# Norms, running sums and output tiles of a two-layer encoder placed among chains of matmuls

## The chip, the cores and the metric

The kernel runs on one core of a Trainium2 chip. It is one inference step, and what is measured is the device time of one execution in microseconds (us). The core has five engines that take their instructions from queues of their own: PE (matmuls, and their weight loads, PEld), DVE (vector work), ACT (activations), POOL (GpSimd: elementwise work here) and SP (here it issues the transfers between memory and the core). An engine takes its queue in order; a semaphore tells it when what another engine makes is there.

## The reference

Two layers work on 2048 tokens of a prompt and 32 tokens of a sample, 1024 numbers each, all in f32:

```python
sh, sc, gt = split(silu(c) @ ada_w[i] + ada_b[i])            # modulation, once per sequence
h = rmsnorm(x, norm_pre[i]) * (1 + sc) + sh
# layer 0: RG-LRU, 12 blocks of 128 channels
xb, gate = split(h @ w_in)                                   # 1024 -> 2 x 1536
xc = conv4(xb); r, ig = sigmoid(xc @ w_a + b_a), sigmoid(xc @ w_x + b_x)
hs = scan(a = exp(-8 r softplus(-lam)), u = sqrt(1 - a*a) * ig * xc)
y = (hs * silu(gate)) @ w_out
# layer 1: forgetting attention, 16 heads of 64
q, k, v, g, fl = split(h @ w_in); log_f = log_sigmoid(fl + b_f)
cum = cumsum(log_f)                                          # the sample starts from 512 cached rows
y = (softmax(q k / 8 + cum_q - cum_k, causal) @ v * silu(g)) @ w_out
x = x + gt * rmsnorm(y, norm_post[i])                        # after each layer
```

Outputs are x of both sequences, the states of layer 0, and k, v and log_f of layer 1.

## The kernel before

Every f32 operand of a product is split into a rounded part (hi) and the rest (lo), and one product is three matmuls, hi·hi, lo·hi and hi·lo. The helpers at L92 to L101 are these splits: `hi` on ACT, POOL or DVE, `lo` always a subtraction on DVE.

The tokens go in two halves of 1024; the second half carries the 32 sample tokens as well. The stages in order of time:

- Setup and modulation of layer 0: `ada` (L227) streams the modulation weights in 512-column pieces, splits them (tiles `scs`) or takes them whole (`scf`) and multiplies at L290. The modulation of layer 1's scale, shift and gate is spread over later stages.
- `prenorm` (L309) of a half: groups of two token tiles of 128 tokens are loaded (L326), ACT takes the sum of squares (L335), DVE and POOL make the factor (L337 to L339) and DVE scales the rows (L342). Then eight blocks per group, one for each 128 of the 1024 channels: two transposes on PE (L361) into a bank of PSUM, ACT scales and shifts it out of the bank (L367), POOL makes hi (L95) and DVE lo (L101). The result is `h`, the moving operand of the layer's products.
- `lru_in` for a half: twelve blocks of weights; for each chunk of up to 512 tokens a chain of 24 matmuls for xb and one of 24 for the gate (L460), then the convolution (L483), the gates' matmuls (L473) and the tail with the scan (L494 to L511) of the block before. The gate weights lie in two slots (`wg`).
- `load_wout` (L566) splits the output weights; `out_tiles` (L586) multiplies each of 17 token tiles by them (L624: 12 pairs of k, six matmuls each), normalizes, adds the residual (L638 to L647) and stores.
- Layer 1: `prenorm` of a half; `proj` (V at L796, then units k, q, g of eight pairs of heads at L825); `forget` and `forget_sums`, whose matmuls at L696 and L697 are the running sums of the log forget values; `attention` as jobs of a pair's head (products at L990, L1024, L1028, L1076, L1077).
- `merge` (L1238) puts the steps of `main()` (projections, then output tiles) beside those of the attention by a ratio of estimated costs, and a last `out_tiles` follows.

Generators write this order: each function yields between steps, and the main body says which is advanced when. A list scheduler behind it may still move an instruction past others, so the order on an engine is not quite the order of the code. Buffers are named pools (`h` 32, `w` 5, `raw` 3, `half` 5, `ahalf` 12, `c` 12, `wg` 2), and the eight banks of PSUM are pj 2, st 2, mx 2, pva 1 and pvb 1. A new tile waits until the last reader of its slot has ended.

At the borders the old order is: all of a half's groups are normalized in runs of eight blocks (the first two groups before the first products, the rest after the first block), out tiles follow one by one, and the second half's norm begins when the first half's `h` comes free.

## Time and profile before

| | us |
|---|---|
| median of three runs (3147.41 to 3154.5) | 3149.36 |
| profiled execution, its own time | 3159.12 |
| its span (first to last instruction) | 3157.4 |
| PE busy in the span | 2935.5 (93%) |
| PEld | 2340.3 (74%) |
| DVE | 1921.4 (61%) |
| ACT | 1425.5 (45%) |
| POOL | 1372.6 (43%) |

PE is busy nearly all the time, so its time is read in two steps: how long it was busy in a stretch, and which share of its full clock it was granted meanwhile. The share is in the column PEclk of the windows (1.00 is the upper level, 2.4 GHz, 0.50 the lower, 1.2 GHz; what lies between is a mixture). A stretch without waits at full clock has PE busy for all of it and 1.00.

### The profile page before, as it was taken

The page shows a single profiled execution, that of the slowest core. Times are in us where ns is not written, and L with a number is a line of the kernel's source. Part 1 is how long each engine was busy: PE and PEld are TensorE (multiplying, and loading weights), DVE is VectorE, ACT ScalarE, POOL GpSimd, SP SyncE. Part 2 cuts the span into 40 slices and gives each one's busy share as a digit, 9 for nine tenths or more (in the row PEclk, how much of TensorE's full clock was granted, in tenths as well). Part 3 has the DMA queues.
Part 4 walks back from the last instruction along what each step waited for, and adds up shares of the span by engine and source line. Part 5 has one row for each costly group of instructions (what it writes and reads, how often), then busy time and mean ns, then how long its engine had stood idle before and what let it go on. Part 6 is the DMA issues. An engine that isn't in the chain of part 4 may idle for free.

```text
span 3157.4 us, 45059 instructions
## 1 busy us (share of the span) xinstructions
PE 2935.5 (93%) x14900; PEld 2340.3 (74%) x14900; DVE 1921.4 (61%) x3387; ACT 1425.5 (45%) x2884; POOL 1372.6 (43%) x1449
## 2 busy tenths in 40 slices
PE   7999899998999999999998989999999989888988
PEld 3777678896678877777776777777878777766667
DVE  7787657757322556554655747676676766675732
ACT  4455555555111424343435616464555646454621
POOL 6444243323121534343444515564555555454632
PEclk9999889999999999999999889999999999988999
DMA  8545424333533476776757563455455445444333
GB/s 280 170 166 183 167 96 137 125 131 120 176 91 117 158 240 183 223 201 198 213 191 215 158 205 91 132 160 155 123 151 148 129 132 141 134 135 116 84 99 117
DMA packets 341432, 488.72 MB, mean 155 GB/s; under 512 B 79112, under 2 KB 191880, under 8 KB 341200
## 3 DMA queue, kind: packets, MB, share of 16 engines
q1 hardware_dynamic: 341200, 485.85, 50.3%
q8 instruction: 118, 1.93, 0.3%
q14 instruction: 114, 0.93, 0.1%
HBM read 307.57 MB, written 178.14 MB: 154 GB/s over the span
## 4 chain that ended last, share of the span: by engine, by line
PE 28%; issue 6%; DVE 6%; DMA 5%; POOL 3%; ACT 2%; SPq 1%; POOLq 0%; DVEq 0%; ACTq 0%
PE pj L825 8%; PE st L1024 3%; PE pva L1076 3%; PE mx L990 3%; PE st L1028 3%; PE pvb L1077 2%; PE pj L796 2%; PE pj L624 2%; DVE ahalf L101 1%; POOL ahalf L1053 1%; DVE mxs L993 1%; POOL half L646 1%; DMA dns_d<-rc 1%; ACT ahalf L1030 1%; DVE half L101 1%
## 5 line engine op out<-in xcount | busy, mean ns | idle before, releaser
L1053 POOL TENSOR_TENSOR ahalf<-ahalf,ahalf 128x512 f32<-128x512 f32 (+2 forms) x528 | 578.4, 1095 | 321.0 <-ACT ahalf L1030 296.1
L825 PE MATMUL pj<-h,w 128*128 128x512 f32 (+1 forms) x2304 | 597.4, 367 | 9.3 <-DVE w L101 8.0
L101 DVE TENSOR_TENSOR ahalf<-st,ahalf 128x512 fp32r<-128x512 f32 (+3 forms) x640 | 386.3, 605 | 247.1 <-ACT st L1031 196.1
L1030 ACT ACTIVATE ahalf<-st 128x512 fp32r<-128x512 f32 (+3 forms) x640 | 340.9, 533 | 379.6 <-PE st L1028 333.8
L825 PEld LDWEIGHTS pj<-h,w 128*128 128x128 f32 x2304 | 427.5, 192 | 93.9 <-DVE w L101 9.7
L993 DVE TENSOR_REDUCE mxs<-mx 128x1 f32<-128x512 f32 (+5 forms) x672 | 384.7, 595 | 100.6 <-PE mx L990 71.6
L1031 ACT ACTIVATE st<-st 128x512 f32<-128x512 f32 (+2 forms) x720 | 354.9, 493 | 0.0
L1024 PE MATMUL st<-ahalf,kv 128*128 128x512 f32 (+3 forms) x640 | 251.6, 395 | 50.8 <-DVE ahalf L101 41.1
L990 PE MATMUL mx<-kb,qm 96*128 96x512 f32 (+5 forms) x672 | 250.1, 398 | 19.0 <-DVE mxs L993 14.1
L796 PE MATMUL pj<-w,h 128*128 128x256 f32 (+3 forms) x1296 | 246.0, 294 | 0.0
L1028 PE MATMUL st<-ahalf,kb 96*128 96x512 f32 (+3 forms) x640 | 243.1, 389 | 2.4 <-ACT ahalf L1011 2.0
L1076 PE MATMUL pva<-ahalf,vs 128*128 128x512 f32 (+3 forms) x640 | 235.0, 387 | 6.4 <-ACT ahalf L1030 4.5
L1077 PE MATMUL pvb<-ahalf,vs 128*65 128x512 f32 (+3 forms) x640 | 227.7, 368 | 8.4 <-DVE ahalf L101 7.4
L101 DVE TENSOR_TENSOR ahalf<-ahalf,ahalf 128x512 fp32r<-128x512 f32 (+1 forms) x163 | 142.5, 877 | 148.8 <-PE st L624 97.0
L101 DVE TENSOR_TENSOR half<-half,half 128x256 fp32r<-128x256 f32 (+3 forms) x160 | 140.3, 877 | 150.3 <-POOL half L95 142.7
L95 POOL TENSOR_SCALAR half<-half 128x256 fp32r<-128x256 f32 (+3 forms) x160 | 85.5, 535 | 330.4 <-ACT half L833 127.2
L460 PE MATMUL pj<-h,w 128*128 128x512 f32 (+1 forms) x1056 | 228.2, 367 | 0.8 <-POOL h L95 0.7
L460 PEld LDWEIGHTS pj<-h,w 128*128 128x128 f32 x1056 | 182.9, 192 | 36.0 <-POOL h L95 1.2
L796 PEld LDWEIGHTS pj<-w,h 128*128 128x128 f32 (+1 forms) x1296 | 197.5, 190 | 12.5 <-ACT half L367 0.2
L1024 PEld LDWEIGHTS st<-ahalf,kv 128*128 128x128 f32 x640 | 123.0, 192 | 98.9 <-DVE ahalf L101 64.4
L624 PE MATMUL pj<-h,w 128*128 128x512 f32 (+1 forms) x624 | 180.3, 427 | 14.7 <-DVE half L645 9.2
L825 PE MATMUL pj<-h,raw 128*128 128x272 f32 (+1 forms) x576 | 191.6, 333 | 0.0
(315 smaller groups left out, 5733.2 us busy)
## 6 DMA issues: line engine op xcount, KB each, us to landing
wp_d<-w SPq DMA_DIRECT2D x60, 512.0 KB
vs<-v_d SPq DMA_DIRECT2D x96, 256.0 KB
kv<-k_d SPq DMA_DIRECT2D x192, 128.0 KB
ahalf<-q_d SPq DMA_DIRECT2D x192, 128.0 KB
raw<-in_w SPq DMA_DIRECT2D x44, 512.0 KB
ahalf<-in_ada_w SPq DMA_DIRECT2D x64, 256.0 KB
v_d<-half SPq DMA_DIRECT2D x64, 256.0 KB
w<-wp_d SPq DMA_DIRECT2D x30, 512.0 KB
```

The source lines that it names most:

```text
L101: dve.tensor_tensor(o, i, f(h), ALU.subtract)
L460: pe.matmul(ps[:, :b - a], l, cols(r, a, b), start=i == 0, stop=i == 23)
L796: pe.matmul(ps[:m, :nw], l, r, start=c == 0, stop=c == 23)
L825: pe.matmul(ps[:, :b - a], l, cols(r, a, b), start=c == 0, stop=c == 23)
L990: pe.matmul(ps[:sw, :kw], u.qm[0:96, s0:s0 + sw], kb, start=True, stop=not last)
L993: dve.tensor_reduce(u.mxs[:sw, si, c:c + 1], ps[:sw, :kw], axis=AX.X, op=ALU.max)
L1024: pe.matmul(ps[:kw, c0:nq], j.ka[k0 // 512][:, kc:kc + kw], u.qa[:, c0:nq], start=True, stop=False)
L1028: pe.matmul(ps[:kw, c0:nq], j.kb[k0 // HALF][0:96, kd:kd + kw], u.qb[0:96, c0:nq], start=False, stop=True)
L1030: act.activation(ph[:kw, c0:nq], ps[:kw, c0:nq], AF.Exp, scale=0.125)
L1031: act.activation(ps[:kw, c0:nq], ps[:kw, c0:nq], AF.Exp, scale=0.125)
L1053: pool.tensor_tensor(u.acc[:kw, c0:nq], f(ph)[:kw, c0:nq], u.acc[:kw, c0:nq], ALU.add)
L1076: pe.matmul(u.pva[:, c:nq], vs[:kw, 0:128], ph[:kw, c:nq], start=ti == 0, stop=last)
```

## The change

The norm gets a written plan. `prenorm` reads a string: `L01` loads groups 0 and 1, `S01` makes their statistics and scales them, `R01:a` runs their blocks for the first four k (`:b` for the last four), `Y` gives the turn back. A function says in which pool each row lies, and a block is one step. `weave(gen, other, n)` advances `other` by n steps behind each step of `gen`; `take` advances a generator by a number of steps.

- *Start.* `ada` for scale and shift is cut in two: pieces 0 and 2 run first, 1 and 3 between the blocks of groups 0 and 1. The first block's chains come in quarters (two k each), xb and gate in turn, between the blocks of the second four k. Groups 2 and 3 are woven into the second chunk.
- *Half switch of layer 0.* Loads, statistics and scaling of the second half's first groups stand before or in the last block; its second chunk is woven with two blocks behind each quarter chain. Chunks of half 1 are cut 512, 256, 288 and no longer 512, 272, 272.
- *Modulation of layer 1's gate* moves from the out tiles (whole f32 products) into the modulation that runs beside the chains (split products).
- *Out tiles, layer 0.* The first two tiles run together on each pair of weights, in four banks. The norm of layer 1's first half is woven into the last tile's twelve steps and into the first sixteen steps of V.
- *Running sums.* Their DVE part (`prepare`) stands at the end of V; the matmuls come after the first k unit, those of the sample after the first q unit.
- *Half switch of layer 1.* Statistics before the last unit; two blocks behind each of its steps, then one behind each of 24 steps of V.
- *Attention and end.* In half 1 the sample's two jobs come before the pair's long ones. `main()` does seven out tiles in place of eight; the last call does tile 7, tiles 8 to 15 and the sample tile, in place of the sample tile and 8 to 15.

```diff
-ADA_FIRST, ADA_LAST = 8, 6
-
-NORM_AT, NORM_WITH = 15 * 12, 8
-
-V_STEPS = 8
+ADA_FIRST = 8
+
+NORM_AT, NORM_WITH = 14 * 12, 12
...
-    return [(0, 512), (512, 784), (784, 1056)]
+    return [(0, 512), (512, 768), (768, 1056)]
...
-    def prenorm(layer, half, src, h, bank, xn_role=lambda g: "xn"):
+    def prenorm(layer, half, src, h, bank, plan, row, by_k=False):
...
+        for step in plan.split():
+            gs = [int(c) for c in step[1:].split(":")[0]]
+            if step[0] == "L":
+                load(gs)
+            elif step[0] == "S":
+                stats(gs)
+            elif step[0] == "Y":
+                yield 0.0
+            else:
+                ks = range(4, KD) if step.endswith("b") else range(4) if step.endswith("a") else range(KD)
+                for gi, k in [(gi, k) for k in ks for gi in gs] if by_k else [(gi, k) for gi in gs for k in ks]:
+                    yield block(gi, k)
+                if not step.endswith("a"):
+                    flags.update(("n", layer, half, gi) for gi in gs)
...
+    def weave(gen, other, n):
+
+        i = 0
+        while True:
+            try:
+                x = next(gen)
+            except StopIteration as e:
+                return e.value
+            yield x
+            for _ in range(n[i % len(n)]):
+                x = next(other, None)
+                if x is not None:
+                    yield x
+            i += 1
+
+    def take(gen, n):
+        for _ in range(n):
+            x = next(gen, None)
+            if x is not None:
+                yield x
...
-        def chain(ps, wh, wl, a, b):
-            i = 0
-            for k in range(KD):
+        def chain(ps, wh, wl, a, b, ks):
+            for k in ks:
                 lh = wh[:, 128 * k:128 * k + 128]
                 ll = wl[:, 128 * k:128 * k + 128]
-                for l, r in ((lh, h[0][k]), (lh, h[1][k]), (ll, h[0][k])):
-                    pe.matmul(ps[:, :b - a], l, cols(r, a, b), start=i == 0, stop=i == 23)
-                    i += 1
+                for i, (l, r) in enumerate(((lh, h[0][k]), (lh, h[1][k]), (ll, h[0][k]))):
+                    pe.matmul(ps[:, :b - a], l, cols(r, a, b), start=k + i == 0, stop=k == KD - 1 and i == 2)
...
+            if n == NB - 1:
+                flags.add(("last", 0, half))
+                yield 0.0
...
-                ps = bank()
-                chain(ps, wxh, wxl, a, b)
-                for (u, v, c) in spans(a, b):
-                    act.activation(xb[:, 3 + c:3 + c + v - u], ps[:, u:v], AF.Copy)
-                ps = bank()
-                chain(ps, wgh, wgl, a, b)
+                px, pg = bank(), bank()
+                first = n == 0 and ci == 0
+                parts = [(px, wxh, wxl), (pg, wgh, wgl)]
+                order = [(q, p) for q in range(4) for p in parts] if first else [(q, p) for p in parts for q in range(4)]
+                for i, (q, p) in enumerate(order):
+                    chain(*p, a, b, (2 * q, 2 * q + 1))
+                    if q == 3 and p is parts[0]:
+                        for (u, v, c) in spans(a, b):
+                            act.activation(xb[:, 3 + c:3 + c + v - u], px[:, u:v], AF.Copy)
+                    if i < 7:
+                        yield 0.0
+                ps = pg
+                del px, pg, p, parts, order
...
+        groups = [[i] for i in range(len(tiles))]
+        if both:
+            groups[0:2] = [[0, 1]]
+        for i in groups[0]:
+            load(i)
+            split(i)
+        for gi, g in enumerate(groups):
+            nxt = groups[gi + 1] if gi + 1 < len(groups) else []
+            for i in nxt:
+                load(i)
+            pss = [[bank(), bank()] for _ in g]
+            xs = []
+            for k in range(kn):
+                wh, wl = w[0][k], w[1][k]
+                for i, ps in zip(g, pss):
+                    m = rows(tiles[i])
+                    o = zq[i][k // kz]
+                    zh, zl = o[0][:, k % kz, :], o[1][:, k % kz, :]
+                    for c, (l, r) in enumerate(((zh, wh), (zh, wl), (zl, wh))):
+                        for n in range(2):
+                            pe.matmul(ps[n][:m, :], l, r[n], start=k + c == 0, stop=k == kn - 1 and c == 2)
...
-        sums(fl, lsum, [128] * 8, ext_d, HALF * half)
+        parts = prepare(fl, lsum, 8)
+        yield
+        sums(parts, [128] * 8, ext_d, HALF * half)
+        del parts
...
-                if kind == "k" and p == 0:
-                    forget_sums(half, fl, bank)
-                    yield 2000.0
+                if kind in "kq" and p == 0 and ("f", half) not in flags:
+                    next(fsum, None)
...
+                for sample in ((True, False) if half else (False,)):
...
-        pre = prenorm(0, 0, io["x"], h, bank1)
+
+        pre = prenorm(0, 0, io["x"], h, bank1, "L01 S01 Y R01:a L23 R01:b S23 Y R23",
+                      lambda g, t: ("xn", "xn") if g < 2 else ("aw", "xn"), by_k=True)
         next(pre)
-        run(ada(0, (0, 2, 1, 3), bank0, bank0, ADA_FIRST, lambda i: i % 3 == 0))
+        mod = ada(0, (0, 2, 1, 3), bank0, bank0, ADA_FIRST, lambda i: i % 3 == 0)
+        left = [lambda: None, lambda: None]
+        blocks = lru_in(0, h, bank0, bank1, lc, left)
+        run(take(mod, 2 * KD))
+        for i in range(KD):
+            run(take(mod, 2))
+            run(take(pre, 1))
+            if i == KD // 2:
+                next(blocks)
+        run(mod)
+        next(blocks)
+        for _ in range(4):
+            run(take(pre, 2))
+            next(blocks)
+        run(until(pre, ("n", 0, 0, 0)))
...
             yield from ada(1, (0, 1, 2, 3), bpvb, bank0)
+            yield from ada(1, (4, 5), bpvb, bank0)
...
+        run(take(weave(take(blocks, 4), pre, (4, 4, 4, 4)), 99))
+        run(pre)
+        run(side(until(blocks, ("last", 0, 0))))
+        h = new_h()
+        pre = prenorm(0, 1, io["x"], h, bank1, "L01 S01 L2 Y R01:a S2 R01:b L3 Y R2 L4 S3 Y R3 S4 R4",
+                      lambda g, t: {(0, 0): "raw", (0, 1): "raw", (1, 0): "raw", (2, 1): "w"}.get((g, t), ("xn", "xn")),
+                      by_k=True)
+        next(pre)
+        second_half = lru_in(1, h, bank0, bank1, lc, left)
+        next(second_half)
+        run(until(blocks, ("free", 0, 0, 0)))
+        run(weave(blocks, pre, (2,)))
+        run(until(pre, ("n", 0, 1, 0)))
+        blocks = second_half
+        run(take(blocks, 2))
+        run(weave(take(blocks, 7), pre, (1, 2)))
+        run(until(pre, ("n", 0, 1, 2)))
+        run(weave(side(take(blocks, 8)), pre, (2,)))
+        run(pre)
+        run(side(until(blocks, ("free", 0, 1, 0))))
         for _ in range(4):
             next(wout)
-        for fn in rest:
+        run(blocks)
+        run(mod)
...
+        pre = prenorm(1, 0, x1_d, h, bank1, "L0 S0 L1 Y S1 R0 L2 R1 S2 L3 Y R2 S3 R3",
+                      lambda g, t: "wg" if g % 2 == 1 else "any")
+        set_roles(big, "half", N_HALF, "z")
+        out = out_tiles(list(range(8)) + [16] + list(range(8, 16)), NB, z_d, io["x"], x1_d, gps, bank0, w, both=True)
+        n_out = 16 * NB
+        run(take(out, NORM_AT))
+        next(pre)
+        run(take(out, n_out - NORM_AT - NORM_WITH))
+        run(weave(out, pre, (1,)))
         del w, gps, out
         run(until(pre, ("n", 1, 0, 1)))
         pbank = [bank0]
         first_half = proj(0, h, lambda: pbank[0]())
-        for part in (until(pre, ("n", 1, 0, 2)), pre):
-            for _ in range(V_STEPS):
-                next(first_half)
-            run(part)
+        run(weave(take(first_half, 16), pre, (1,)))
+        run(pre)
...
+        yield from until(a, ("last", 1, 0))
+        pre = prenorm(1, 1, x1_d, hb, bpj, "L0 S0 L1 Y S1 R0 L2 R1 Y S2 R2 L3 L4 S3 S4 R34",
+                      lambda g, t: "raw" if g == 0 or (g, t) == (1, 0) else ("hf", "hf") if g == 4 else "w")
+        next(pre)
         yield from until(a, ("free", 1, 0, 0))
-        pre = prenorm(1, 1, x1_d, hb, bpj, lambda g: "raw" if g % 2 else "w")
+        yield from weave(a, pre, (2,))
         yield from until(pre, ("n", 1, 1, 1))
-        yield from a
+        yield from weave(take(b, 24), pre, (1,))
...
-        yield from out_tiles(list(range(8)), NP, z2_d, x1_d, y_o, gps, bpj, w, False)
+        yield from out_tiles(list(range(7)), NP, z2_d, x1_d, y_o, gps, bpj, w, False)
...
-    run(out_tiles([16] + list(range(8, 16)), NP, z2_d, x1_d, y_o, att["gps"], cycle(bpj, bpj, bst, bst), att["w"]))
+    run(out_tiles([7] + list(range(8, 17)), NP, z2_d, x1_d, y_o, att["gps"], cycle(bpj, bpj, bst, bst), att["w"]))
```

On PE at the half switch of layer 0, before (st and pj are banks with a chain of products, `ident` marks a transpose, `scs` a modulation product):

```order
L460 MATMUL st_3259<-h_839,wg_2791 128x512
L460 MATMUL st_3259<-h_840,wg_2791 128x512
L460 MATMUL st_3259<-h_839,wg_2792 128x512
L290 MATMUL pvb_2513<-ahalf_2997,scs 34x512
L290 MATMUL pvb_2513<-ahalf_2998,scs 34x512
L361 MATMUL pva_3055<-ident,ahalf_3005 128x128
L361 MATMUL mx_3064<-ident,ahalf_3005 128x128
L361 MATMUL mx_3073<-ident,ahalf_3005 128x128
```

The first transposes of the second half follow the last product of the first half's last chain. After the change, in the last block's second chunk:

```order
L361 MATMUL mx_3068<-ident,raw_2927 128x128
L361 MATMUL mx_3068<-ident,ahalf_2929 128x128
L497 MATMUL pj_3051<-h_775,w_2792 128x512
L497 MATMUL pj_3051<-h_791,w_2791 128x512
L497 MATMUL pj_3051<-h_792,w_2791 128x512
L497 MATMUL pj_3051<-h_791,w_2792 128x512
L361 MATMUL mx_3081<-ident,raw_2923 128x128
L361 MATMUL mx_3081<-ident,raw_2925 128x128
L361 MATMUL pva_3090<-ident,raw_2927 128x128
```

Products of the last chains (L460, now L497) stand between the transposes.

On DVE at the same place, before (c tiles belong to the last blocks of `lru_in`, ss and rs to the norm):

```order
L101 TENSOR_TENSOR c_3293<-c_3287,c_3292 128x1024
L533 COPY c_3520<-convc 128x3
L534 COPY c_3520<-cst 128x3
L535 MEMSET c_3520 128x1
L497 SCALAR_TENSOR_TENSOR c_3297<-c_2975,c_3297 128x1024
L337 TENSOR_TENSOR ss_3021<-ss_3021 128x2
L338 TENSOR_SCALAR rs_3022<-ss_3021 128x2
L342 TENSOR_SCALAR ahalf_3005<-ahalf_3005,rs_3022 128x512
```

The norm's factor and its scaling stand behind the convolution and part of the tail of the last blocks. After the change:

```order
L592 TENSOR_TENSOR c_2544<-c_2544,st_2652 128x512
L99 TENSOR_TENSOR wg_2610<-raw_2396,wg_2609 128x1024
L99 TENSOR_TENSOR c_2719<-c_2713,c_2718 128x1024
L571 MEMSET c_2735 128x3
L533 SCALAR_TENSOR_TENSOR c_2723<-c_2621,c_2723 128x1024
L345 TENSOR_SCALAR rs_2934<-ss_2933 128x2
L349 TENSOR_SCALAR raw_2923<-raw_2923,rs_2934 128x1024
L349 TENSOR_SCALAR raw_2925<-raw_2925,rs_2934 128x1024
```

The scaling (now L349, whole rows) stands one block earlier, ahead of the last block's own work (c_2735).

## Rows read from the trace of the kernel before

**Rows 1.** Windows by stage: length; busy us (instructions) per engine; PEclk, DMA share, GB/s

```profile
80.00:370.00 290.00, 289.00 (x1243) 229.25 (x1242) 220.47 (x196) 140.66 (x162) 117.53 (x82) 1.00 0.52 176
0.00:80.00 80.00, 57.28 (x209) 28.89 (x210) 61.86 (x141) 34.18 (x75) 54.43 (x77) 0.91 0.80 279
370.00:440.00 70.00, 48.07 (x199) 34.27 (x198) 40.54 (x85) 45.10 (x92) 29.76 (x50) 0.71 0.27 89
750.00:860.00 110.00, 96.72 (x350) 65.40 (x351) 59.13 (x78) 37.44 (x59) 28.90 (x23) 0.91 0.57 177
1060.00:1140.00 80.00, 73.20 (x442) 64.08 (x441) 46.97 (x105) 27.09 (x57) 41.59 (x71) 0.96 0.62 216
1140.00:1720.00 580.00, 541.50 (x2818) 431.14 (x2817) 338.05 (x624) 239.62 (x514) 247.21 (x271) 0.99 0.67 204
1720.00:1900.00 180.00, 158.68 (x877) 130.08 (x876) 104.39 (x242) 74.38 (x159) 65.44 (x99) 0.86 0.61 179
2780.00:3060.00 280.00, 246.92 (x1050) 182.26 (x1051) 164.07 (x321) 129.13 (x303) 141.72 (x145) 0.90 0.38 104
```

**Rows 2.** Timeline of PE at the start: begin, duration, instruction, [wait <- releaser]

```profile
12.26 0.47 PE L361 MATMUL mx<-ident,ahalf 128*128 128x128 f32 x1 [12.26 <-DVE ahalf L342]
...
54.68 7.02 PE L460 MATMUL pj<-h,w 128*128 128x512 f32 x24
```

**Rows 3.** Windows of 10 us at the start

```profile
30.00:40.00 10.00, 9.75 (x41) 3.37 (x40) 9.04 (x15) 2.86 (x6) 10.00 (x10) 1.00 1.01 380
40.00:50.00 10.00, 4.61 (x18) 1.87 (x18) 9.93 (x15) 2.23 (x5) 10.00 (x8) 0.85 0.38 109
```

**Rows 4.** Groups by form, 20 to 58 us: count | busy, mean ns | idle before

```profile
L101 DVE TENSOR_TENSOR c<-h,c 128x512 fp32r<-128x512 f32 x18 | 15.8, 906 | 1.0 <-PE pj L290 0.5 <-POOL c L95 0.4
...
L95 POOL TENSOR_SCALAR h<-ahalf 128x256 fp32r<-128x256 f32 x16 | 11.7, 752 | 0.0
...
L101 DVE TENSOR_TENSOR h<-ahalf,h 128x256 fp32r<-128x256 f32 x16 | 9.3, 639 | 0.3 <-POOL h L95 0.3
```

**Rows 5.** Timeline of DVE at the half switch of layer 0

```profile
384.45 1.67 DVE L342 TENSOR_SCALAR ahalf<-ahalf,rs 128x512 f32<-128x512 f32 x4 [0.80 <-POOL rs L339]
...
391.21 0.41 DVE L101 TENSOR_TENSOR h<-ahalf,h 128x256 fp32r<-128x256 f32 x1
```

**Rows 6.** Waits of PE, 370 to 440 us: us in total, times, longest

```profile
PE pva L361 <- DVE ahalf L342: 9.2, 1, 9.2
PE mx L361 <- ACT ahalf L367: 6.3, 5, 2.3
PE pva L361 <- ACT ahalf L367: 6.0, 3, 2.7
```

**Rows 7.** PE groups by form over the span: the later modulation

```profile
L290 PE MATMUL pvb<-ahalf,scs 128*34 128x512 f32 x96 | 30.2, 394 | 0.0
...
L290 PE MATMUL pvb<-ahalf,scf 128*34 128x512 f32 x32 | 15.4, 599 | 0.0
```

**Rows 8.** Windows of 10 us at the entry of the out tiles

```profile
760.00:770.00 10.00, 10.00 (x44) 7.32 (x42) 9.96 (x12) 7.79 (x12) 3.57 (x4) 1.00 0.31 105
770.00:780.00 10.00, 5.58 (x12) 2.75 (x11) 10.00 (x9) 5.08 (x6) 7.89 (x4) 0.71 0.46 159
```

**Rows 9.** Window of 20 us at the half switch of layer 1

```profile
1840.00:1860.00 20.00, 11.51 (x65) 9.14 (x66) 10.75 (x39) 0.40 (x1) 0.42 (x1) 0.57 0.58 178
```

**Rows 10.** Waits of PE, 1680 to 1900 us

```profile
PE pj L696 <- DVE fg L98: 7.4, 2, 4.2
```

**Rows 11.** Timeline of PE at the end

```profile
3029.23 12.91 PE L624 MATMUL pj<-h,w 128*128 128x512 f32 x48 [2.91 <-DVE half L645]
...
3047.19 12.84 PE L624 MATMUL pj<-h,w 128*32 128x512 f32 x48 [5.05 <-ACT w L92]
```

**Rows 12.** Windows of 10 us: transposes among modulation products, and among out tiles' products

```profile
420.00:430.00 10.00, 7.90 (x27) 5.24 (x27) 6.16 (x17) 7.09 (x18) 6.57 (x14) 0.50 0.08 19
1090.00:1100.00 10.00, 9.98 (x76) 9.70 (x75) 8.52 (x21) 6.38 (x15) 7.62 (x15) 0.92 0.39 142
```

242 lines of the change are left out of this document (111 added, 131 removed).

## The prediction

> **What bounds the kernel now.** The windows by stage come first. Each row gives PE's busy time and the clock it was granted; a stretch's length less busy time times clock is what it lost against a full-clock PE that never waits. In 80:370, the dense middle of layer 0's first half, that is 290 − 289.0 × 1.00 = 1.0 us, and 1243 matmuls in 289 us make 0.23 us for one (mostly 512 columns). Where stages meet, the rows [rows 1] give:
> - 0:80 (start): 80 − 57.28 × 0.91 = 27.9
> - 370:440 (half switch, layer 0): 70 − 48.07 × 0.71 = 35.9
> - 750:860 (entry of the out tiles): 22.0
> - 1060:1140 (layer change): 9.7
> - 1720:1900 (half switch, layer 1): 43.5
> - 2780:3060 (end of attention): 57.8, while the ordinary mix of 1140:1720 loses 43.9 of 580, 7.6%.
>
> So PE is the bound and the borders are where it is not fed. Then the waits and timelines of each border say what came last there.
>
> **The change, part by part.** The instruction work is nearly the same (17 more PE rows of 14,700), so each term is a share of a border's loss.
>
> *1, start.* The first transpose runs at 12.26 [rows 2]: that much of the 27.9 is load and setup, which stay. 15.6 are in play. The first product chain ran whole at 54.68, after the modulation. Now it comes in quarters, between the halves of the norm's blocks, and two modulation slices precede the other two. Half of the chain's 48 products, 5.5 us, can run in time that PE waited, and about 2.5 of the wait in 40:50 (PE 4.61 of 10) goes with it: 8 us. Against more: DVE and POOL are at 9 to 10 of 10 from 30 to 50 [rows 3], and what they split is the same, so they go on setting this stretch's end. The loads of token groups 2 and 3 now stand on SP's queue behind all of block 0's split weights; the chunk that needs them runs a whole chunk later, 11 us, which covers them. If that cover fails the term is nothing. Bounds 0 and 15.6.
>
> In 20:58 the same split of 128x256 took 639 ns on DVE with POOL's `hi` at 752 ns beside it [rows 4], and 0.41 us when POOL was idle [rows 5]. The Trainium skill ("SBUF — State Buffer", SBUF: two separate sides) says that a DVE operation with two SBUF inputs and a GpSimd operation that reads SBUF exclude each other through one port pair. By that rule the two engines are one resource here and no order of PE's work helps: the term would be 0 to 2 and the sum 67. The rows bear it in direction (the slower pair), not as a full lock, since both ran above 9 of 10 busy.
>
> *2, half switch of layer 0.* PE waited 9.2 us for the first normalized tile, then 6.3 and 6.0 for the ScalarE copies that give the transposes' banks back [rows 6]; with 0.3 of small ones 21.8, the remaining 14 is the clock (0.71). The first wait is DVE's doing: L342 ran at 384.45, behind the tail of the last block, 1.67 us for four, with a wait for POOL's power of 0.80 [rows 5]. Now loads, statistics and scaling of the first groups stand within the last block, and its second chunk has two blocks of transposes behind every six products: 9.2 goes, and most of the bank waits, since 1.4 us of products lies between two pairs. What is late next: block 0's gate weights for half 1 must wait until the last gate chain gives their slots back (1.05 MB at the 380 GB/s of [rows 3], 2.8 us, plus their splits on POOL and DVE), and the last eight blocks of the second group still come without cover. I leave 12 of 35.9 for these: 24 us gained. Bounds 12 (only the waits' half) and 33 (all but the weights).
>
> The Trainium skill ("Perfetto Trace Analysis", Identifying the Most-Contended Engine) holds matmul busy time for a bad measure and takes weight-load busy time instead. By that, dense work loads weights 229.25/290 = 0.79 of the time, 370:440 holds 34.27/0.79 = 43.4 us of such work and lost 26.6, not 35.9; the term would be 15 and the sum 65. I keep the first, since the measured waits and the clock row add up to it.
>
> *3, entry of the out tiles.* The last row before the products is full on DVE (9.96 and 10.00 of 10) while PE falls to 5.58 [rows 8]: the split of the output weights, one pair per k, sets the pace of the first tile. Two tiles on each pair bring 12 × 6 × 0.23 = 16.6 us of products into that stretch. The modulation of layer 1's gates goes from whole f32 products (32 rows, 15.4 us) to split ones (32 rows more, at 30.2/96 = 0.315: 10.1 us) [rows 7]: 5.3 less. Against it: ten of these slices now come after the last chain, and each splits 128x512 on DVE, 10 × 0.9 [rows 4] = 9 us into an engine that is full there. 16.6 + 5.3 − 9 = 12.9, I take 12. Bounds −4 (the splits cost 9 and the second tile is no cover) and 27 (all of the 22.0 and the 5.3).
>
> *4, layer change.* 9.7 lost; the norm's first two groups are woven into the last tile's twelve steps, the rest one block a step into V. The old code did the same in bulk, at a clock of 0.96. I take 4, bounds −4 and 9.7.
>
> *5, half switch of layer 1.* At the ordinary 7.6%, 180 us lose 13.7; the excess is 29.8. Of it 1840:1860 lost 20 − 11.51 × 0.57 = 13.4, with 7.4 us of waits of the running sums of the forget gates for their DVE splits, 2 of them, the longest 4.2 [rows 9, 10]. The first sums keep their place on PE but are prepared at the end of V, a whole k unit earlier; the sample's move behind q. But the longest wait is for the head of a DVE queue that stays: I take 7 of the 13.4. The rest, 16.4, is the bare run of 72 transposes before V; two blocks a step in the last unit and one in 24 V steps take most: 11. Together 18, bounds 5 and 28.
>
> *6, end.* After the last attention matmul the old order has 56 + 432 products, and the tile matmuls at 3029.23 and 3047.19 waited 2.91 and 5.05 and took 12.91 and 12.84 for 48 where 48 × 0.23 makes 11.0 [rows 11]: 11.7 in play. Now tile 7 stands there in place of the small sample tile, which ends the list, so first splits have more cover. The last finish is of 32 rows, not 128, on the same engines. 8, bounds 0 and 12.
>
> *7, attention.* Sample jobs now precede the long ones of each pair; the same units, the same pace rule. The 57.8 of 2780:3060 is 36 above the ordinary share, and nothing added reaches the ScalarE–DVE–POOL chain there. 0, bounds −25 and +15.
>
> Sum: 8 + 24 + 12 + 4 + 18 + 8 + 0 = 74. The profiled execution took 3159.1 us, 9.8 above the median of the runs, 3149.4. 3159.1 − 74 = 3085; on the median's base **3075**.
>
> **The rivals.** (a) *The waits move into the chains.* DVE and POOL have the same splits and scalings to do; woven, each block's wait for its ScalarE copy or its bank stands in front of products, as the waits of 6.3 and 6.0 did [rows 6]. For it: both engines near full at three of the borders. Against: in 80:370 products with the same engines behind them ran dense [rows 1]. Terms 2, 3 and 5 give half or less: about 31, 3118.
>
> (b) *All of it is recovered*: 15.6 + 30 + 20 + 8 + 24 + 8 = 105, 3044. For it: dense stretches lose 0.3%. Against: weights that come late, and stretches bound by DVE.
>
> (c) *Slower: the clock falls in the woven stretches.* Woven products: the last block of half 0 and the first of half 1, 22 and 23 us, the last out tile 17, V's 16 and 24 steps of six half-width products, 11 and 17, the first chain 11: 101 us. At 1.2 in place of 2.4 GHz each costs itself once more. Gains that need no clock: 8 (term 1), 14 (term 2 less 10 of clock), 12, 7 and 8: 49. The change loses once more than 49/101 = 48% of these stretches run at the lower level; at 70% it is 3149.4 + 71 − 49 = 3171. For it: 420:430, transposes between products of the modulation, shows PE busy 7.90 of 10 and a clock of 0.50. Against: 1090:1100, transposes among the out tiles' products, busy 9.98 at 0.92 [rows 12].
>
> (d) *No effect*: DVE and POOL bind at every border and all comes back later: 3149.
>
> **How the numbers follow.** Main case 0.56, (a) 0.20, (b) 0.12, (c) 0.07, (d) 0.05. The main case's own range is 3055 to 3095, some terms at a bound and not all at the same one. For 8 in 10 the range takes in (b) with terms near their upper bounds and (a) down to a third of the gain: 3038 to 3130; left out are (c), (d) and the tails. 0.2% is 6.3 us, about what a measurement of this kernel tells from no change. Faster holds for the main case, (a) and (b): 0.88; same 0.05; slower 0.07.
>
> **What would show it.** After the change, the half switch of layer 0 should hold no wait of PE over 4 us and a clock above 0.85 over its 70 us; the first out tiles should run at PE over 9 of 10; the two sums' waits should be below 4 together; the last tiles should wait under 3. Term 1 is wrong if PE stays under 6 of 10 in a slice before 60 us. The whole is wrong if the lower clock covers woven blocks (c), or if the stages are as short as said and attention between 1900 and 3060 is longer by more than 25 us.

## The result: slower, and where the profile after shows it

The changed kernel took 3186.3 us in the median of three executions, the kernel before, run beside it, 3151.9: by the means 1.0113 of its time, 95% interval 1.0087 to 1.0140. A fourth execution took 9458.5 us for a reason that no trace shows and is left out. 3075 with a range of 3038 to 3130 was predicted; the direction was wrong.

The windows by stage of the changed kernel, in the columns of [rows 1] (length; busy us and instructions of PE, PEld, DVE, ACT, POOL; PEclk, DMA share, GB/s):

```profile
80.00:370.00 290.00, 288.05 (x1236) 226.53 (x1236) 222.71 (x209) 146.04 (x175) 119.87 (x93) 1.00 0.51 174
0.00:80.00 80.00, 53.59 (x188) 24.52 (x188) 56.16 (x132) 29.88 (x66) 45.44 (x65) 0.91 0.75 264
370.00:440.00 70.00, 55.73 (x253) 39.88 (x251) 52.87 (x89) 42.02 (x81) 38.51 (x55) 0.83 0.35 116
750.00:860.00 110.00, 82.40 (x305) 61.29 (x306) 63.44 (x81) 35.04 (x54) 43.46 (x27) 0.80 0.50 159
1060.00:1140.00 80.00, 70.40 (x427) 60.91 (x426) 49.01 (x108) 30.72 (x64) 42.12 (x72) 0.96 0.59 204
1720.00:1900.00 180.00, 154.46 (x850) 124.51 (x850) 100.14 (x235) 75.84 (x165) 66.35 (x104) 0.90 0.55 158
```

Only 370:440 improved by much: it lost 70 − 55.73 × 0.83 = 23.7 where [rows 1] gave 35.9. The start lost 31.2 against 27.9, the entry of the out tiles 44.1 against 22.0, the layer change 12.4 against 9.7, the half switch of layer 1 41.0 against 43.5.

Windows of equal place mislead once a stage has moved, so the rest is read by marks: the start of the same product, counted along the products of one line, in the timelines of both kernels. The table gives the place of each mark and, below a kernel's name, how much longer (+) or shorter (−) than in the kernel before the stretch up to it was. "Three", "l0 in bulk" (bulk_l0) and "scratch" (before_hf) are experiments below.

| mark | before at | changed | three | l0 in bulk | scratch |
|---|---|---|---|---|---|
| 1105th chain product (last block of half 0) | 363.4 | +5.9 | +0.9 | +1.3 | +4.7 |
| 2017th (half 1, seventh block) | 586.8 | −10.4 | −8.1 | −12.9 | −16.2 |
| end of the last chain | 747.9 | +5.0 | +5.8 | +4.8 | −0.1 |
| 289th out-tile product | 856.5 | +7.0 | −29.4 | −26.9 | +1.0 |
| 193rd product of layer 1's projections | 1110.3 | +2.1 | +1.8 | +1.9 | +1.8 |
| 1825th | 1696.1 | +1.2 | −1.6 | −3.2 | −5.5 |
| 2401st (behind the half switch) | 1906.1 | +0.7 | +0.9 | +0.2 | −2.5 |
| end of the last product at L1076 (L1156 in the changed kernel) | 3023.6 | +19.6 | +1.9 | −8.8 | −7.4 |
| end | 3157.4 | +1.8 | −5.9 | −6.5 | −0.2 |
| sum (profiled spans) | | +32.9 | −33.7 | −50.1 | −24.4 |

How exact a mark is: before_jobs below differs from the kernel before only from attention's half 1 on, and its marks agree with it to 1.4 us up to 1696. In attention the same order of instructions can differ by some 10 us (last section), so there the medians decide. A few attention products still follow the last one at L1076: in the kernel before they end 0.8 us behind it, in the changed kernel 4.0. Counted from the very last, the changed kernel's attention is 22.8 us longer and its end 1.4 shorter.

*Entry of the out tiles.* The chains end at 748.5, the first out-tile product starts at 783.1; before it was 747.9 and 749.9. Waits of PE from 748 to 800 us in the changed kernel (total, times, longest):

```profile
PE pvb L288 <- DVE ahalf L99: 7.1, 5, 4.1
PE pvb L288 <- DVE ahalf L251: 7.0, 1, 7.0
PE pj L698 <- DVE ahalf L99: 4.7, 1, 4.7
PE pj L698 <- ACT ahalf L90: 3.2, 1, 3.2
```

and its windows of 10 us there:

```profile
750.00:760.00 10.00, 3.25 (x7) 1.19 (x7) 8.81 (x11) 5.02 (x7) 4.99 (x6) 0.68 0.77 258
760.00:770.00 10.00, 7.05 (x20) 4.66 (x19) 7.63 (x11) 7.24 (x10) 10.00 (x6) 0.50 0.38 115
770.00:780.00 10.00, 4.07 (x9) 1.48 (x8) 10.00 (x12) 4.41 (x7) 6.95 (x5) 0.50 0.30 97
780.00:790.00 10.00, 2.21 (x5) 1.30 (x5) 10.00 (x12) 6.12 (x8) 6.84 (x3) 0.50 0.51 175
```

L288 is the modulation. Ten of its slices (20 products) stand behind the last chain; PE waits for their splits one by one, and once 7.0 us for DVE to read the bank of the piece before (L251), at the lower clock, with DVE full from 770 on. The out tiles' own splits take their tiles from the same pool, `ahalf`, and come last. The timeline of DVE and POOL shows what a split cost there (begin, duration):

```profile
775.42 3.27 POOL L532 TENSOR_TENSOR c<-c,c 128x1060 f32<-128x1060 f32 x1 [2.49 <-ACT c L510]
776.39 2.84 DVE L99 TENSOR_TENSOR ahalf<-ahalf,ahalf 128x512 fp32r<-128x512 f32 x1
```

The split of 128x512, 0.9 in [rows 4], took 2.84 us and ended 0.54 after the POOL operation that began before it. That is what the Trainium skill ("SBUF — State Buffer", SBUF: two separate sides) says of a DVE operation with two SBUF inputs beside a GpSimd one that reads SBUF: the second waits for the whole of the first. This row agrees. The wait is not shown as one: the row counts as busy for all of its 2.84 us, so a full DVE is not all work.

*Start.* Modulation and chain did begin earlier (first chain product at 40.9, not 54.68), and then PE stood for a scaling of groups 2 and 3. Its timeline:

```profile
63.40 1.32 PE L497 MATMUL pj<-h,w 128*128 128x512 f32 x5
70.20 0.45 PE L361 MATMUL pva<-ident,h 128*128 128x128 f32 x1 [5.49 <-DVE h L349]
```

The window of 10 us there:

```profile
60.00:70.00 10.00, 4.71 (x23) 3.54 (x21) 3.11 (x10) 6.47 (x19) 3.51 (x6) 0.87 1.00 361
```

and the queue of SP (begin and duration of an issue):

```profile
46.19 4.78 SPq L483 DMA_DIRECT2D wl_d<-wg  x2
56.78 0.32 SPq L484 DMA_DIRECT2D wt_d<-half  x1
57.15 0.42 SPq L327 DMA_DIRECT2D h<-in_x  x1
```

The rows' loads are issued at 57.15, behind the last store of block 0's weights; in the kernel before the first four stood ahead of two of them.

### The profile page after: what moved, and what is told of

It reads as the page before. It is cut to its first block, busy times and chain, and to the rows that moved or that the text cites. A ratio compares the mean times of both kernels' runs of the same rounds, so it can differ in the third digit from the quotient of the medians.

```text
span 3190.3 us, 45115 instructions
## 1 busy us (share of the span) xinstructions
PE 2942.4 (92%) x14900; PEld 2343.3 (73%) x14900; DVE 1944.0 (61%) x3405; ACT 1422.2 (45%) x2878; POOL 1389.1 (44%) x1465
## 4 chain that ended last, share of the span: by engine, by line
PE 32%; DMA 6%; DVE 6%; issue 5%; POOL 4%; ACT 2%; SPq 1%; POOLq 0%; DVEq 0%; ACTq 0%
PE pj L907 9%; PE mx L1070 3%; PE st L1104 3%; PE pj L698 3%; PE st L1108 3%; PE pva L1156 3%; PE pj L876 3%; PE pvb L1157 2%; POOL ahalf L1133 2%; DVE ahalf L99 2%; PE st L698 1%; DVE mxs L1073 1%; DMA od<-dn_d 1%; ACT ahalf L1110 1%; DMA rc<-dns_d 1%
## 5 line engine op out<-in xcount | busy, mean ns | idle before, releaser
L907 PE MATMUL pj<-h,w 128*128 128x512 f32 (+2 forms) x2304 | 603.8, 370 | 15.4 <-DVE w L99 10.1
L1111 ACT ACTIVATE st<-st 128x512 f32<-128x512 f32 (+3 forms) x720 | 354.9, 493 | 0.0
L1156 PE MATMUL pva<-ahalf,vs 128*128 128x512 f32 (+3 forms) x640 | 235.6, 389 | 4.7 <-ACT ahalf L1110 2.8
L497 PE MATMUL pj<-h,w 128*128 128x512 f32 (+2 forms) x1056 | 235.8, 370 | 2.8 <-DVE h L99 1.7
L497 PEld LDWEIGHTS pj<-h,w 128*128 128x128 f32 x1056 | 183.8, 192 | 41.1 <-DVE h L99 4.3
L907 PE MATMUL pj<-h,raw 128*128 128x288 f32 (+2 forms) x576 | 194.6, 338 | 0.0
L497 PE MATMUL st<-h,wg 128*128 128x512 f32 (+2 forms) x840 | 189.7, 377 | 0.1
L1070 PEld LDWEIGHTS mx<-kb,qm 96*128 96x128 f32 (+1 forms) x672 | 127.8, 194 | 82.7 <-DVE mxs L1073 54.3
```

What stands on the lines that cost most here:

```text
L497: pe.matmul(ps[:, :b - a], l, cols(r, a, b), start=k + i == 0, stop=k == KD - 1 and i == 2)
L907: pe.matmul(ps[:, :b - a], l, cols(r, a, b), start=c == 0, stop=c == 23)
L1070: pe.matmul(ps[:sw, :kw], u.qm[0:96, s0:s0 + sw], kb, start=True, stop=not last)
L1111: act.activation(ps[:kw, c0:nq], ps[:kw, c0:nq], AF.Exp, scale=0.125)
L1156: pe.matmul(u.pva[:, c:nq], vs[:kw, 0:128], ph[:kw, c:nq], start=ti == 0, stop=last)
```

## Experiments

Every kernel ran in five rounds beside the kernel before, on one of four chips; ratios are to the kernel before of the same rounds, and kernels of different rounds are compared by them. Theory A and the rival are those of the expectation that stands above each result.

**mod_ahead, jobs_back, loads_early, three.** Edits of the changed kernel:

```diff
# mod_ahead: in side(), beside the later chains (AHEAD is 26)
+                    turn[0] += 1
+                    if turn[0] > AHEAD and turn[0] % 2:
+                        next(mod, None)
# jobs_back
-                for sample in ((True, False) if half else (False,)):
+                for sample in ((False, True) if half else (False,)):
# loads_early: the norm's plan reaches L23 before the first weights are split
         run(mod)
+        run(take(pre, 2))
         next(blocks)
-        for _ in range(4):
+        next(blocks)
+        for _ in range(3):
```

> The changed kernel with one edit: beside the later chains of layer 0's second half every other chunk advances the modulation by two slices, so none is left after the last chain. Theory A (ten modulation slices after the last chain hold back the out tiles: their splits stand in DVE's and POOL's queues ahead of the output weights' splits, and their buffers are those of the tiles' splits; 35 us from the last chain to the first out-tile product): that gap falls below 12 us and the time by 18 to 26 us from 3189. Rival (the output weights' splits and the last block's tail fill DVE there anyway): the gap moves into the first two tiles, gain 0 to 6 us.

3152.5 us, ratio 1.0008 (0.9993 to 1.0023): 33 us below the changed kernel (1.05% of the kernel before), more than either theory said. The first out-tile product follows the chains at once (753.2). Its windows of 10 us:

```profile
750.00:760.00 10.00, 8.92 (x50) 7.51 (x48) 7.64 (x11) 5.45 (x10) 3.27 (x3) 1.00 0.64 214
760.00:770.00 10.00, 9.54 (x44) 7.80 (x45) 10.00 (x11) 9.35 (x11) 6.16 (x5) 1.00 0.36 117
770.00:780.00 10.00, 8.85 (x39) 6.66 (x37) 7.00 (x11) 7.25 (x10) 6.32 (x4) 1.00 0.40 149
```

PE is at 9 of 10 and full clock where it stood at 2 to 7 and half clock. From the end of the chains to the 289th out-tile product it takes 80.9 us; the changed kernel 115.5, the kernel before 108.6. The slices themselves cost 5 us beside the chains, whose end comes at 753.4 and no longer at 748.5.

> The changed kernel with the old order of attention jobs in half 1 (a pair's two long jobs, then the sample's two). Theory A (the new order costs what the stretch from 1900 us to the end of attention grew by, about 20 us): 16 to 24 us faster than 3189. Rival (that stretch grew because the projections beside it were paced or woven otherwise): 0 to 5 us faster.

3167.1 us, 1.0054 (1.0037 to 1.0071): 19 us below the changed kernel (0.59% of the kernel before). Theory A.

> The changed kernel, but token groups 2 and 3 are loaded ahead of the stores of block 0's split weights on SP's queue. Theory A (PE's wait of 5.5 us near 65 us, and the cold clock behind it, is for these loads): 5 to 8 us faster than 3189, and that wait gone. Rival (DVE and POOL set the start's end in any order): 0 to 2 us.

3188.0 us, 1.0118 (1.0096 to 1.0139), the changed kernel's time. The marks show 3.3 us gained at the start, the wait of 5.5 is 1.9; it is too small for the medians. Rather the rival.

> The changed kernel with all three edits. Theory A: the gains add, 40 to 55 us, so 3134 to 3149, at or below the 3152 of the kernel before. Rival (the losses share one cause and are not additive): 10 to 25 us, so 3164 to 3179.

3125.8 us, 0.9928 (0.9908 to 0.9948): by the ratios 58 us below the changed kernel, where the three alone gave 33, 19 and nothing. The gains add, a little more than Theory A had it, and the kernel beats the one before.

**before_jobs, sample_mid.** The first puts the change's job order (the diff of the change) into the kernel before; the second is "three" with the sample's jobs in the middle:

```diff
-                for sample in ((False, True) if half else (False,)):
-                    for e in range(2):
+                for e0, sample in (((0, False), (0, True), (1, True), (1, False)) if half else ((0, False), (1, False))):
+                    for e in (e0,):
```

> The kernel before with one edit: in half 1 the sample's two attention jobs stand before the pair's long ones. Theory A (the order of jobs costs by itself, wherever the projections stand): 18 to 28 us slower than the kernel before, 3170 to 3180. Rival (it costs only together with the woven projections): within 6 us of 3151.5.

3177.8 us, 1.0076 (1.0056 to 1.0096): 24 us slower by this edit alone. Theory A.

> Three edits, with a pair's two sample jobs between its two long ones. Theory A (a pair that begins with its sample jobs needs its fresh q, k, v earlier, so only the head of a pair is the bad place): within 5 us of the three-edit kernel. Rival (any place other than behind both long jobs costs, by what then runs beside what): 12 to 28 us slower.

3137.8 us, 0.9968 (0.9957 to 0.9979): 0.40% above "three", 13 us. The rival, at the low end of its figure: the head of a pair is not the only bad place. Windows between the 2401st product of the projections and their end, changed kernel first, then jobs_back:

```profile
1917.60:2824.60 907.00, 841.42 (x4602) 681.24 (x4601) 614.40 (x1192) 478.13 (x1094) 482.93 (x514) 0.96 0.50 138
```

```profile
1919.80:2802.40 882.60, 826.04 (x4562) 667.99 (x4562) 605.63 (x1171) 474.80 (x1086) 479.98 (x510) 0.97 0.49 138
```

PE stood idle for 907.0 − 841.42 = 65.6 us against 56.6, 9 more; part of the rest is the clock (0.96 against 0.97). The other pair that differs in this order alone, the kernel before and then before_jobs:

```profile
1906.10:2786.40 880.30, 825.24 (x4564) 667.78 (x4563) 607.42 (x1173) 475.65 (x1087) 479.87 (x510) 0.98 0.49 138
```

```profile
1898.40:2800.70 902.30, 831.39 (x4604) 671.13 (x4603) 620.58 (x1193) 478.60 (x1093) 483.54 (x514) 0.98 0.49 138
```

Here 16 of the 22 us are idle time (70.9 against 55.1), at the same clock. So more idle time of PE is what both pairs show, and the clock is no part of it in one. It is a little in many places, no one wait. Why this phase of sample jobs against projections is worse stays open.

**one_tile, old_end.** "Three" with one part undone:

```diff
# one_tile; NORM_AT and n_out follow the added group
-        out = out_tiles(list(range(8)) + [16] + list(range(8, 16)), NB, z_d, io["x"], x1_d, gps, bank0, w, both=True)
+        out = out_tiles(list(range(8)) + [16] + list(range(8, 16)), NB, z_d, io["x"], x1_d, gps, bank0, w)
# old_end
-        yield from out_tiles(list(range(7)), NP, z2_d, x1_d, y_o, gps, bpj, w, False)
+        yield from out_tiles(list(range(8)), NP, z2_d, x1_d, y_o, gps, bpj, w, False)
...
-    run(out_tiles([7] + list(range(8, 17)), NP, z2_d, x1_d, y_o, att["gps"], cycle(bpj, bpj, bst, bst), att["w"]))
+    run(out_tiles([16] + list(range(8, 16)), NP, z2_d, x1_d, y_o, att["gps"], cycle(bpj, bpj, bst, bst), att["w"]))
```

> The kernel with three edits (modulation ahead of the last chain, old job order, loads first; 3125.8 us), but the first two out tiles one after the other. Theory A (two tiles on each pair of weights cover the weights' splits, and that is most of the 30 us gained at the entry): 12 to 18 us slower, the second tile's products end that much later. Rival (the entry is fast because the modulation is gone from it): 0 to 4 us slower.

3142.3 us, 0.9958 (0.9940 to 0.9976). The entry takes 91.8 us (79.3 in "three"): the pair gives 12.5. Theory A by the marks (by the ratios 9 us, with intervals that overlap); the other 17 of 29 come from the modulation that is gone, whose whole products took 15.4 us of this stretch [rows 7].

> Three edits, with eight out tiles in the main stream and the sample tile first in the last call, as before. Theory A (the end's new order is worth the 6 us by which the stretch behind the last attention product is shorter in the three-edit kernel, 8 predicted): 4 to 8 us slower. Rival (that stretch only got shorter because tile 7 was moved out of the attention's time): within 2 us.

3130.4 us, 0.9945 (0.9932 to 0.9958), 0.17% slower, within the intervals of both; by the marks the end takes 134.6 us against 127.9. Theory A, weakly.

**bulk_l1, bulk_l0, all_bulk.** "Three" without the weave at the half switch of layer 1, of layer 0, of both. The norm runs in bulk again; its scratch tiles stay in the change's pool:

```diff
# bulk_l0
-        run(side(until(blocks, ("last", 0, 0))))
+        run(side(until(blocks, ("free", 0, 0, 0))))
         h = new_h()
-        pre = prenorm(0, 1, io["x"], h, bank1, "L01 S01 L2 Y R01:a S2 R01:b L3 Y R2 L4 S3 Y R3 S4 R4",
+        pre = prenorm(0, 1, io["x"], h, bank1, "L01 S01 Y R0 L2 R1 L3 Y S23 R2 L4 S4 R3 R4", lambda g, t: ("xn", "xn"))
...
-        run(weave(blocks, pre, (2,)))
+        run(until(pre, ("n", 0, 1, 1)))
+        run(blocks)
# bulk_l1
-        yield from until(a, ("last", 1, 0))
...
-        yield from weave(a, pre, (2,))
         yield from until(pre, ("n", 1, 1, 1))
-        yield from weave(take(b, 24), pre, (1,))
+        yield from a
         yield from pre
```

> The kernel with three edits, but the norm of layer 1's second half in bulk as before, not woven. Theory A (the weave at this border moved PE's waits and gained nothing: between the marks on either side of it the three-edit kernel needs 1 us more than the kernel before): within 5 us of 3125.8. Rival (it gains the 11 us predicted for the transposes, lost again at the running sums): 8 to 14 us slower.

3122.8 us, 0.9899 (0.9880 to 0.9919). No slower than "three" (0.9908 to 0.9948): the rival falls, the weave there gained nothing.

> Three edits, with the norm of layer 0's second half in bulk as before. Theory A (the weave at this border is worth the 10 us that the marks around it show, less than the 24 predicted): 8 to 14 us slower than the three-edit kernel (ratio 0.9955 to 0.9972). Rival (it is worth the whole 24, and something else in the same stretch lost 14): 20 to 28 us slower.

3109.8 us, 0.9887 (0.9872 to 0.9903). Faster, not slower: both theories were wrong. Some 5 us of it lie at the switch by the marks; the rest is in attention, whose order is the same. The stretch behind the switch, first "three", then bulk_l0:

```profile
400.00:450.00 50.00, 40.27 (x193) 29.63 (x192) 37.50 (x62) 27.17 (x53) 24.23 (x36) 0.83 0.39 127
```

```profile
400.00:450.00 50.00, 47.38 (x274) 39.36 (x273) 35.80 (x70) 35.11 (x69) 24.95 (x39) 1.00 0.33 112
```

Woven, the chains' products wait behind blocks whose scaling is late; in bulk they run at full clock here. Just before it is the other way round: from 350 to 400 the clock is 0.97 woven and 0.86 in bulk. Over both stretches 100 − 85.65 × 0.90 = 22.9 us are lost woven and 100 − 87.77 × 0.93 = 18.4 in bulk.

> Three edits, and the norms of the second halves of both layers in bulk. Theory A (both weaves cost more than they hide): as fast as bulk_l0 or up to 8 us faster, ratio 0.986 to 0.989. Rival (the gains of bulk_l0 and bulk_l1 lie in how the attention's timing happened to fall, and do not add): ratio 0.990 to 0.993.

3115.0 us, 0.9895 (0.9880 to 0.9910): between the two figures, and as bulk_l0. The two do not add.

**before_hf.** If not the weave, then what cured the switch? The kernel before with one line:

```diff
         set_roles(big, "h", N_H, "aw")
+        set_roles(big, "half", N_HALF, "hf")
```

> The kernel before with one edit: the scratch tiles of the norm (hf) come from the pool half, not from the pool ahalf that holds the token rows. Theory A (at the half switch of layer 0 the rows had to wait for slots that scratch tiles and modulation held, and this is what the change cured): PE's wait of 9.2 us for DVE's scaling goes and that switch is 8 to 14 us shorter; the start, whose first transposes now come later, loses some of it again; in all 3 to 12 us faster than before. Rival (the weave, the chunks' quarters or the earlier statistics did it): the switch within 3 us of before.

3137.0 us, 0.9967 (0.9954 to 0.9980). The switch is 16.2 us shorter, the start 4.7 longer. Waits of PE from 350 to 460 us, in the changed kernel and in before_hf:

```profile
PE mx L361 <- DVE raw L349: 3.4, 1, 3.4
PE mx L361 <- DVE ahalf L349: 3.3, 2, 2.3
PE pj L497 <- DVE h L99: 1.7, 1, 1.7
```

```profile
PE pva L361 <- ACT half L367: 5.6, 2, 5.0
PE mx L361 <- ACT half L367: 5.6, 4, 3.7
PE mx L361 <- ACT half L335: 0.6, 1, 0.6
```

The wait of 9.2 for L342 of [rows 6] is gone without any weave. The token rows had shared twelve slots of `ahalf` with the norm's scratch tiles and the modulation. With the scratch tiles elsewhere, the fourth load of rows is issued at 354.37 us and no longer at 364.27, the first statistics run at 344.54 and no longer at 378.39, and the first scaling, at 384.45 in [rows 5], is done before the last chain has begun:

```profile
362.23 1.67 DVE L342 TENSOR_SCALAR ahalf<-ahalf,rs 128x512 f32<-128x512 f32 x4 [0.58 <-POOL rs L339]
```

Theory A.

**old_start, best, new_start_hf, old_start2.** The start of the kernel before in "three" (old_start), in bulk_l1 (best) and in bulk_l0 (old_start2); and the new start in bulk_l0 with the scratch tiles in `ahalf` until it is over (new_start_hf):

```diff
# best and old_start2, with the first chain whole and scratch tiles in ahalf until this norm is over; old_start has "L01 S0 Y S1 R0 L2 S2 R1 L3 Y S3 R2 R3"
+        pre = prenorm(0, 0, io["x"], h, bank1, "L01 S01 Y R0 L2 R1 L3 Y S23 R2 R3", lambda g, t: ("xn", "xn"))
         next(pre)
+        run(ada(0, (0, 2, 1, 3), bank0, bank0, ADA_FIRST, lambda i: i % 3 == 0))
# new_start_hf
-        set_roles(big, "half", N_HALF, "hf")
         setup()
...
         run(pre)
+        set_roles(big, "half", N_HALF, "hf")
```

> The kernel with three edits, but with the start in the old order: modulation in one run, norm blocks of groups 0 and 1 before the first chain, that chain whole, groups 2 and 3 behind it. Theory A (DVE and POOL set the start in any order, the trace shows block 1 of layer 0 at 89.6 us against 87.8): between 3 us faster and 2 us slower. Rival (the split modulation and the quartered chain gain what was predicted, and something else at the start takes it): 5 to 10 us slower.

3141.5 us, 0.9955 (0.9939 to 0.9971), which looks like the rival, but the kernel was no copy of the old start: a load that waited for a slot held up SP's queue and delayed weights behind it. Inconclusive, so best followed.

> Three edits, the norm of layer 1's second half in bulk, and the start of the kernel before, row for row on PE. The kernel old_start was no clean copy of that start (its loads of groups 2 and 3 stood ahead of the weights and PE waited 14.2 us for modulation weights), so this one takes its place. Theory A (the new start, with its loads put right, is worth nothing: block 1 of layer 0 at 89.6 to 91.3 us against 87.8 before): block 1 at 87 to 89, the time within 4 us of bulk_l1 (ratio 0.988 to 0.991). Rival (the new start pays the predicted 8 us somewhere behind block 1): 6 to 10 us slower than bulk_l1.

3121.0 us, 0.9916 (0.9903 to 0.9930); block 1 at 86.9. The interval takes in part of both theories' figures (to 0.991; 0.992 to 0.993); by the marks theory A.

> The fastest kernel so far (three edits, layer 0's second half in bulk; ratio 0.9887), with the norm's scratch tiles of the start in the pool of the token rows, as before; afterwards in their new pool. Theory A (the lost us of the start are for the scratch tiles' pool of five): block 1 of layer 0 at 83 to 87 us, so 1 to 5 us earlier than before and 3 to 6 earlier than in the fastest. Rival (POOL and DVE, or the loads, set it): at 88 to 91.

3113.2 us, 0.9891 (0.9870 to 0.9912), block 1 at 90.2: the rival. The scratch pool is not what holds the new start.

> The same kernel with the start of the kernel before. Block 1 at 86 to 88 us by either theory, and 1 to 4 us faster than bulk_l0 if what is won at the start stays won: ratio 0.987 to 0.990.

3110.8 us, 0.9886 (0.9864 to 0.9907), block 1 at 86.8. With every other part equal the old start is 3.4 us earlier than the new; the medians can't tell the two, nor either from bulk_l0.

So the change holds a version that beats both kernels: bulk_l0, 0.9887 of the time before, without its weave at layer 0's switch, its job order, its late modulation and its late loads.

## Why the prediction was wrong, by its own steps

Forecast and measured, changed kernel, in us of the marks: start −8 and +5.9; half switch of layer 0 −24 and −10.4; entry −12 and +7.0, with +5.0 in the chains ahead of it; layer change −4 and +2.1; half switch of layer 1 −18 and +1.9 (1.2 + 0.7); end −8 and +1.8; attention 0 and +19.6. The sum was −74 and is +32.9. Three edits that undo the late slices, the job order and the late loads take 58 us back, so they hold more than all of the loss; the other terms are gains that came smaller or not at all.

*Attention (term 7) failed in its reason.* "The same units, the same pace rule" was taken to mean the same time. before_jobs shows 24 us for the order alone. The value 0 had no row under it, and the measured 19.6 lies outside the bounds given (−25 and +15).

*Entry (term 3): mechanism right, one size wrong.* The pair of tiles gives 12.5 (16.6 was its share). "10 × 0.9 = 9 us" for the late slices priced only DVE's time, at a duration from another stretch. They cost 115.5 − 80.9 = 34.6: each is a chain of load, POOL, DVE and PE that stands ahead of the next stage's own splits. Lengthened splits (2.84 us) and the lower clock are part of that. The 5.3 for cheaper products did not come either: the 128 products took 45.5 us in the changed kernel, 30.2 + 15.4 before; with the slices ahead (mod_ahead) they took 40.2. Without late slices the out tiles' stretch is 27.7 shorter than before, but that is not the term: 15.4 of it are products that only left the stretch, and 10.1 come back in the chains. What is left, 12.5 + 5.3 = 17.8, is more than the 12 taken. The +5.0 in the changed kernel's chains is such a part: from the 2017th product to the chains' end it has 32 modulation products, the kernel before 16, and 16 at 0.315 us are 5.0.

*Half switch of layer 0 (term 2): right that the wait for L342 goes, wrong why.* It went because scratch tiles left the rows' pool (before_hf, −16.2). The weave on top takes some 5 us away again (−12.9 in bulk, −8.1 woven in "three"; with the old start, in old_start2 and best, −12.8 and −7.9). Against −16.2 stand more modulation products in this stretch, 50 in bulk_l0 and 46 in "three" where before_hf has 36; at 0.315 us each, an estimate from [rows 7], bulk_l0's switch is as good as that of before_hf. The term read a wait for DVE and looked only at what stood before it on DVE, not at when the rows could be loaded. The term of 15 by the weight-load rule of the Trainium skill ("Perfetto Trace Analysis", Identifying the Most-Contended Engine) would have been nearer, in its number only: it says nothing of the pool.

*Start (term 1): the sign.* The loads behind the stores were named as the term's risk and called covered; they were not, which is 3 us. The sign named for a failure, PE under 6 of 10 in a slice before 60 us, did not show; the hole came in 60:70 (4.71). With loads and pools put right the new start is still 3.4 us behind the old. What it wins first it loses in the second chunk, which has groups 2 and 3 woven in: in bulk_l0 that chunk begins at 70.7 (73.3 before), and block 1 at 89.6 (87.8 before). A window of bulk_l0 there:

```profile
70.00:80.00 10.00, 9.43 (x40) 7.21 (x41) 6.76 (x13) 5.83 (x12) 7.33 (x15) 0.70 0.09 23
```

DVE and POOL are not full in it; PE is busy at a lower clock. What sets the end of this stretch stays open. The port rule of the Trainium skill ("SBUF — State Buffer", SBUF: two separate sides), set aside at that place, gave 0 to 2 and was nearer than 8. The reason for setting it aside, that both engines ran above 9 of 10 busy, does not speak against it: a split that waits for POOL is shown as busy, as the row of 2.84 us is. That a lock is what held the start is not shown.

*Half switch of layer 1 (term 5): waits moved, as rival (a) had it.* The running sums did stop waiting (0.2 for 7.4 of [rows 10]), and the window of [rows 9], 11 us earlier in the stretch by the marks, is full (the first line). What it lost stands beside it (the second), where 20 − 15.27 × 0.74 = 8.7 us are lost:

```profile
1840.00:1860.00 20.00, 19.85 (x137) 17.93 (x136) 13.78 (x40) 3.08 (x7) 6.94 (x11) 1.00 0.73 213
1800.00:1820.00 20.00, 15.27 (x72) 12.29 (x73) 14.79 (x32) 12.93 (x28) 9.65 (x16) 0.74 0.18 49
```

But from 1700 to 1920 us PE now waits for these (first rows of the list):

```profile
PE pj L907 <- issue: 5.1, 2, 3.6
PE mx L1070 <- DVE mxs L1073: 4.5, 3, 2.4
PE pj L361 <- ACT half L369: 4.1, 10, 0.7
PE st L1104 <- DVE ahalf L99: 3.8, 4, 1.8
```

The stretch is as long as before, and bulk_l1 is no slower.

*Layer change and end (terms 4, 6).* The first lost about 2 in every version of the changed kernel (1.4 to 2.7); before_hf, with the old layer change and the new scratch pool, lost 1.8 there too, so that it was the weave is not shown. The end is worth 5.9 in "three", near the 8, but with the new job order the long jobs come last and it is gone or nearly so.

*Rival (c)*, a lower clock in woven stretches, did not happen as priced: the changed kernel's 370:440 has 0.83 (0.71 before), its layer change 0.96. The lower clock did come at the entry, 0.50 from 760 to 790, where nothing was woven and PE waited for the slices, and in 40:50 and 70:80 of the start (0.68 and 0.78). The time was lost in those waits, which term 3 had at 9 us, and in attention, which the sum had at nothing. (The 17 more PE rows that the prediction counts are none in the traces: both have 14,900.)

## What to carry to other kernels

Price work that is moved to a border by its whole chain and by what it then stands ahead of, not by its busy time on one engine; here the same ten slices cost 5 us beside the chains and 34.6 behind them. Before an order is rewritten to hide a wait, look at whether the data could have been there: a one-line change of a pool did more here than the weave. A reorder of equal work is not free until a run says so.

## What the runs showed that was not expected

On every engine's queue "three" and bulk_l0 have the same order of instructions from the out tiles of layer 0 on, yet from the 2401st product of the projections to the end they took 1247.3 and 1236.0 us: what differed is the moment at which attention started, and nothing else that the traces show. A difference of some 10 us there, in one profile, says nothing about an edit; the ones above are carried by medians (before_jobs 24 us, jobs_back 19, sample_mid 13). The job order is also clear of that spread: this stretch takes 1270 to 1273 us in the four profiles with the sample's jobs first, 1262 with them in the middle and 1236 to 1251 in the other thirteen.

The half clock took in stretches that were far from empty. In the changed kernel the rows 760:770 to 780:790 above are all at 0.50, also where PE was busy 7.05 of 10 us; in mod_ahead the same stretch, busy 8.85 to 9.54, is at 1.00. Part of what looked like a price of slices is a price of that clock: from 750 to 790 PE stood idle for 23.4 us and lost another 3.25 × 0.32 + 13.33 × 0.50 = 7.7 to it.
